# First norm rearranged, and the last down pair by seven block products: a hybrid encoder layer on one core

## The chip, the core and the metric

The kernel runs on one core of one Trainium2 chip. The metric is the device time of one execution in microseconds (us). TensorE (PE) does the matrix products into PSUM banks, VectorE (DVE) and ScalarE (ACT) do elementwise work and read the banks, GpSimd (POOL) does some elementwise work and issues some transfers, SyncE (SP) issues most transfers.

## What is computed

One step of an encoder layer for 512 prompt tokens and 64 sample tokens of running streams, 576 in all, with 1024 features. In short:

```
h = LN1(alpha*x + 0.5*FFN1(x))                    # FFN(x) = (silu(x@Wg) * (x@Wu)) @ Wdown, inner width 2816
z = h @ w_in                                       # mLSTM q,k,v,o,i,f | attention q,k,v | two branch gates
h = LN2(alpha*h + w_out(sig(g_m)*P_m(mLSTM(h)) + sig(g_a)*P_a(BandAttn(h))))
y = LN3(alpha*h + 0.5*FFN2(h))
LN(x) = (x - mean) * rsqrt(var + 1e-5) * g + b
```

i and f are the mLSTM's two gates, four heads each: eight columns of `w_in` in all. Attention goes over a band of earlier positions with a learned position bias. The new states of the streams are returned as well.

## The kernel before, in words

**Layout and precision.** Features lie on the 128 partitions, tokens along the free dimension, so the 576 tokens of one block of 128 features are a row of a tile (`T` = 576, `KT` = 8 blocks). Every operand of a matmul is split into a high part in the reduced format fp32r and a low part, the remainder; a product is three matmuls, wh·xh, wh·xl and wl·xh. The high part is a copy by ACT, the low part a subtraction by DVE. For the weights named in `ADDED`, and in some other places, `add_lo` makes the low part without DVE: ACT writes the negated high part, and a transfer issued by POOL adds the source to it. Tokens go in two halves, `HALVES`: 256 + 320 or 320 + 256 columns, or 288 + 288 where block products are used.

**Block products.** Gate/up products, pairs of column tiles (`Units` and its subclasses) and pairs of down tiles (`seven`) use a Strassen–Winograd scheme: a 2×2 block product by seven block products in place of eight. The sums of input blocks that it needs are made by DVE (`Combos`, `Inner`), the sums of weight blocks too (`split_ds`, `prep`). In `seven`, the 22 inner tiles of a down product are 8 (tiles 8 to 15) by block products and 14 by plain products (`plain`); `plan_ffn` lists the weights in the order in which they are loaded.

**Order.** PE's order is written out by hand: `od` counts model time with every group of matmuls (`tick`), and `later(dt, fn)` runs `fn` when that time has come. `od.bg` holds generators that are stepped every so many ns of model time. The other engines' instructions are placed by the scheduler with the priorities that the code gives (`hot`, `high_priority`, `issue_after`). The weights come through two raw buffers (`wr`) and four pairs of split ones (`NWB`).

**A norm.** `Norm.take` adds a product's bank to a tile of the residual `d[j]`, `last` adds tile and square to the running sums, `stats` sums these over partitions by matmuls, `rsqrt` takes the power on POOL, `centre` subtracts the mean from all eight tiles (those in `CP` on POOL), `spread` broadcasts the reciprocal deviation by a matmul and schedules `apply` for each tile: a scaling on DVE, the bias and the high part on ACT, the low part on DVE. The third norm's second half goes another way, transposed (`turned`).

**First norm and the columns after it.** FFN1's last pair of down tiles, 6 and 7, goes by `seven` with a function `first` in the middle, which closes the first half. Of the seven products three go one after the other into bank X, and DVE reads X between them. Then the first column tiles of `w_in` are multiplied in four passes (`WAVE_M`): tiles 0 to 2 of the list for the first half, tile 3, tiles 0 to 2 for the second half, tile 3. The list is 48, 40, 32 (first tiles of attention's v, k and q) and `if`, the gates' columns. They leave their banks as `vf`, `kf`, `qf` and, for the gates, by four ACT operations on 4 partitions (`gate_cb`). The gates' rows are then computed by `gate_rows`, a generator in `od.bg`, while the column pairs (`un.run`) are under way.

**Attention output.** `os_split` splits the attention output and makes the block sums for its projection; for the last three indices POOL begins them (`Combos.begin`), with the two subtractions.

**FFN2's last pair.** Tiles 6 and 7 go by four `gemm`s over all 22 inner tiles, one for each tile and half, and the weights are loaded and split once for each half; the third norm's `spread_at` is 4920.

## Time and profile before

| | us |
|---|---|
| median of 3 runs (lowest to highest) | 1553.24 (1552.8 to 1553.64) |
| the profiled execution | 1553.24 |
| its span in the profile | 1551.5 |
| PE busy | 1530.7 (99%) |
| DVE busy | 1140.2 (73%) |
| ACT busy | 891.7 (57%) |
| POOL busy | 234.7 (15%) |

The span runs from the first to the last recorded instruction. An engine is busy while it executes; waiting is not counted. In the timeline, a row gives the start in us, the busy time, the engine, the code line, the operation, out<-in with the names of tiles, partitions x elements, and how many instructions are joined; in brackets stands how long the engine was idle before it, and what ended that. Matmuls overlap, so a group's busy time is longer than its step, the distance from one start to the next. Line 152 is the helper for elementwise operations of two tiles, 155 the one with a scalar, 149 that for ACT, 135 that for matmuls. A row that begins with two times joined by a colon gives a stretch, its length, busy time and count of PE, PE's weight loads, DVE, ACT and POOL, the granted PE clock, the share of time in which the DMA engines are busy and GB/s.

### The profile page before, as it was taken

The numbers are of one execution on the slowest core, as the hardware profiler recorded it, in microseconds if no ns is written. First come the engines' busy times: TensorE is split into PE (matmuls) and PEld (weight loads), VectorE is DVE, ScalarE is ACT, GpSimd is POOL, SyncE is SP. The second block draws the span as 40 slices with busy tenths as digits, with TensorE's granted clock in tenths as the row PEclk, the third lists the DMA queues.
The fourth block names the chain that finished last, engine by engine and source line by source line (L and its number), as shares of the span: only waits on it lengthen the run. The fifth ranks groups of instructions, "written<-read, shape, count | busy, mean of one in ns | idle before, by whom it ended". The sixth has DMA issues, their size and how long they took to land.

```text
span 1551.5 us, 29498 instructions
## 1 busy us (share of the span) xinstructions
PE 1530.7 (99%) x11579; PEld 1516.1 (98%) x11579; DVE 1140.2 (73%) x2103; ACT 891.7 (57%) x1700; POOL 234.7 (15%) x437
## 2 busy tenths in 40 slices
PE   9999999999999999999999999999999999999998
PEld 9999999999899999999999999999999999999997
DVE  7877778675988766777586766755776877788756
ACT  7544457442866557777754877753456454457333
POOL 1000000000310015555311222202121000001000
PEclk9999999999999999999999999999999999999999
DMA  9232323533754438687534765642755323226334
GB/s 262 108 109 83 105 86 93 142 108 89 204 150 155 137 130 223 153 204 188 120 137 137 189 145 138 163 144 82 210 141 128 109 82 109 82 72 145 119 113 150
DMA packets 80260, 211.15 MB, mean 136 GB/s; under 512 B 9081, under 2 KB 20985, under 8 KB 80121
## 3 DMA queue, kind: packets, MB, share of 16 engines
q1 hardware_dynamic: 65144, 169.15, 33.3%
q0 software_dynamic: 11808, 34.28, 12.7%
q10 hardware_dynamic: 3168, 5.83, 1.1%
q8 instruction: 91, 1.49, 0.4%
q14 instruction: 49, 0.39, 0.1%
HBM read 172.27 MB, written 21.63 MB: 125 GB/s over the span
## 4 chain that ended last, share of the span: by engine, by line
PE 87%; DVE 4%; ACT 4%; DMA 2%; POOL 1%; issue 1%; SPq 0%; ACTq 0%; DVEq 0%; POOLq 0%
PE mm L135 70%; PE aux L135 15%; PE aux L145 2%; DVE s L152 1%; ACT sc L149 1%; DVE wl L152 1%; DVE sc L1585 1%; DMA s<-in_xT 1%; ACT s L149 1%; DMA G<-in_rbias 1%; ACT wh L149 0%; POOL kh L159 0%; DMA wr<-in_w_gu 0%; ACT wh L872 0%; DVE s L155 0%
## 5 line engine op out<-in xcount | busy, mean ns | idle before, releaser
L135 PE MATMUL mm<-s,wh 128*128 128x288 f32 (+2 forms) x3667 | 752.2, 298 | 6.9 <-DVE s L152 3.1
L135 PEld LDWEIGHTS mm<-s,wh 128*128 128x128 f32 x3667 | 588.0, 189 | 11.4 <-DVE s L152 2.3
L135 PE MATMUL mm<-s,wl 128*128 128x288 f32 (+2 forms) x1806 | 533.1, 295 | 0.0
L135 PEld LDWEIGHTS mm<-s,wl 128*128 128x128 f32 x1806 | 340.0, 188 | 0.0
L149 ACT ACTIVATE wh<-wr 128x1024 fp32r<-128x1024 f32 (+2 forms) x143 | 134.0, 948 | 156.7 <-PE mm L135 91.3
L152 DVE TENSOR_TENSOR wl<-wr,wh 128x1024 fp32r<-128x1024 f32 (+2 forms) x93 | 107.5, 1164 | 49.0 <-ACT wh L149 48.6
L135 PE MATMUL mm<-tx,wh 128*128 128x288 f32 x677 | 140.3, 296 | 0.8 <-DVE tx L152 0.8
L135 PEld LDWEIGHTS mm<-tx,wh 128*128 128x128 f32 x677 | 109.2, 188 | 1.2 <-DVE tx L152 1.0
L152 DVE TENSOR_TENSOR wl<-wt,wh 128x1024 fp32r<-128x1024 f32 x51 | 62.5, 1225 | 55.8 <-ACT wh L872 55.8
L135 PE MATMUL mm<-tx,wl 128*128 128x288 f32 x350 | 103.2, 295 | 0.0
L872 ACT ACTIVATE wh<-wt 128x1024 fp32r<-128x1024 f32 x51 | 54.1, 1060 | 83.1 <-DVE wt L152 83.1
L152 DVE TENSOR_TENSOR wl<-wu,wh 128x1024 fp32r<-128x1024 f32 x63 | 77.1, 1223 | 31.3 <-ACT wh L872 31.3
L872 ACT ACTIVATE wh<-wu 128x1024 fp32r<-128x1024 f32 x63 | 66.7, 1058 | 41.2 <-PE mm L135 34.3
L135 PE MATMUL mm<-tx,ah 128*128 128x288 f32 x416 | 85.4, 297 | 0.4 <-ACT st L149 0.4
L198 POOL DMA_DIRECT2D s<-s x16 | 13.7, 854 | 469.4 <-DVE hb L152 426.7
L149 ACT ACTIVATE h<-h 128x288 f32<-128x288 f32 x78 | 34.0, 436 | 60.9 <-DVE h L152 60.9
L135 PEld LDWEIGHTS mm<-tx,ah 128*128 128x128 f32 x416 | 66.2, 188 | 1.2 <-ACT st L149 0.6
L135 PEld LDWEIGHTS mm<-tx,wl 128*128 128x128 f32 x350 | 65.7, 188 | 0.0
L152 DVE TENSOR_TENSOR ws<-wu 128x1024 f32<-128x1024 f32 (+1 forms) x55 | 64.7, 1176 | 0.0
L152 DVE TENSOR_TENSOR wl<-ws,wh 128x1024 fp32r<-128x1024 f32 x51 | 62.2, 1219 | 3.0 <-ACT wh L872 3.0
L135 PE MATMUL mm<-h,wh 128*128 128x288 f32 (+2 forms) x304 | 62.7, 296 | 0.1
L135 PE MATMUL mm<-tx,al 128*128 128x288 f32 x208 | 61.1, 294 | 0.0
(398 smaller groups left out, 3481.8 us busy)
## 6 DMA issues: line engine op xcount, KB each, us to landing
wu<-in_w_gu SPq DMA_DIRECT2D x78, 512.0 KB, 4.4
wr<-in_w_in SPq DMA_DIRECT2D x48, 512.0 KB, 4.2
wr<-in_w_dn SPq DMA_DIRECT2D x37, 512.0 KB, 3.8
wl<-in_w_in POOLq DMA_DIRECT2D x36, 512.0 KB, 6.3
wu<-in_w_in SPq DMA_DIRECT2D x24, 512.0 KB, 4.5
wr<-in_w_dn SPq DMA_DIRECT2D x19, 384.0 KB, 3.2
s<-s POOLq DMA_DIRECT2D x16, 288.0 KB, 4.4
wu<-in_w_ap SPq DMA_DIRECT2D x8, 512.0 KB, 4.7
```

Source lines behind the costliest of these rows:

```text
L135: PE.matmul(out, lhsT, rhs, start=start, stop=stop, **kw)
L145: PE.transpose(out, in_, idn)
L149: return ACT.activation(out, in_, func, **kw)
L152: return (eng or DVE).tensor_tensor(out, a, b, op=op)
L198: return POOL.dma_start(lo, src, accum_op=ALU.add)
L872: self.last = ACT.activation(hi, src, AF.Copy)
L1585: DVE.tensor_tensor_reduce(out=out, in0=ps, in1=g, op0=ALU.add, op1=ALU.min, scale=1.0, scalar=3e38, accum_out=acc)
```

## The change

1. `seven` for FFN1's last pair takes the same order as the others up to q0·t3; a22·t4 goes into a bank R of its own, with one more `take`. The plan of its weights changes to fit.
2. `CP` is empty: all of `centre` on DVE, in all norms.
3. `spread` sets 650 in place of 860 between the tiles of the third norm, the final one; the other norms keep 860.
4. Column tile 32 is last in plan and list; `if` takes its place among the first three; its low part is made by `add_lo`.
5. The first two loads of the column pairs go through `later`.
6. `gate_rows` starts at 30000 in place of 50000, with its first operation behind `un.lo`, a low half of the pairs' weights.
7. `os_split`: all block sums on DVE; three of the eight low halves by `add_lo`.
8. FFN2's last pair goes by `seven` over eight inner tiles, and one `gemm` over the other 14 for both tiles and halves, with the weights held; `spread_at` is 3000.

```diff
-    PIECES = {("in", 48), ("in", 40), ("in", 32)}
+    PIECES = {("in", 48), ("in", 40)}
-    ADDED = {("in", c + j) for c in (32, 40, 48) for j in range(2, KT)} | {("in", c) for c in (*range(2, 8), *range(10, 32), *range(56, 72))} \
+    ADDED = {("in", 32)} | {("in", c + j) for c in (32, 40, 48) for j in range(2, KT)} | {("in", c) for c in (*range(2, 8), *range(10, 32), *range(56, 72))} \
-    CP = (6, 7)
+    CP = ()
...
-            seven(6, "vu")
+            seven(6)
             chunk(6, 0)
             chunk(6, 2)
             return
-        for r in range(2):
-            for j in (6, 7):
-                for c in range(3):
-                    chunk(j, c)
+        seven(6)
+        for j in (6, 7):
+            chunk(j, 0)
+            chunk(j, 2)
...
-    plan_in((48, 40, 32))
+    plan_in((48, 40))
     plan.append(("if", ins["w_if"]))
+    plan_in((32,))
...
-                later(860 * j, lambda j=j: self.apply(j, hf, rb))
+                later((860 if self.final is None else 650) * j, lambda j=j: self.apply(j, hf, rb))
...
-        def begin(self, i):
...
@@ seven
-        if first is None:
-            product(Z, "q1", "t1", True)
-            ln.take(j + 1, B, Z, ALU.subtract)
+        product(Z, "q1", "t1", True)
+        ln.take(j + 1, B, Z, ALU.subtract)
         product(X, "q0", "t3", False, "v")
         ln.take(j + 1, B, X, ALU.subtract)
         if first is None:
             product(Z, "t1", "b22", False, "t")
-        product(X, "a22", "t4", False, "u" if first is None else None)
-        ln.take(j + 1, A, X, ALU.subtract)
-        if first is not None:
+            product(X, "a22", "t4", False, "u")
+            ln.take(j + 1, A, X, ALU.subtract)
+        else:
+            R = bank()[:, :HT_]
+            ln.take(j + 1, A, X, ALU.subtract)
+            product(R, "a22", "t4", True, "u")
+            ln.take(j + 1, A, R, ALU.subtract)
             first()
-            product(Z, "q1", "t1", True, "u")
-            ln.take(j + 1, B, Z, ALU.subtract)
             product(Z, "t1", "b22", False, "t")
...
@@ ffn, the last pair for n == 2
-                    for hf in range(2):
-                        ln.residual(6, hf)
-                    for j, hl in [(j, (hf,)) for hf in (0, 1) for j in (6, 7)]:
-                        gemm([[((f"dn{n}", j, c), nk) for c, (_, nk) in enumerate(DC)]], hp_, [ln.cb(j)], (((0,), hl),))
+                    ln.spread_at = 3000
+                    Y, Z = seven(n, 6, inner, ln)
+                    for ps, cc in ((Y, A), (Z, B)):
+                        ln.take(6, cc, ps, ALU.add)
+                    for j in (7, 6):
+                        ln.whole(j)
...
+                    gemm([[((f"dn{n}", j, c), DC[c][1]) for c in (0, 2)] for j in (6, 7)], Outer(), [ln.cb(j) for j in (6, 7)],
+                         (((0,), (0,)), ((1,), (0,)), ((0,), (1,)), ((1,), (1,))))
...
     def gate_rows():
-        yield stt(t1, fx, -1.0, fx, ALU.mult, ALU.max)
+        with tc.issue_after(un.lo.ins):
+            first = stt(t1, fx, -1.0, fx, ALU.mult, ALU.max)
+        yield first
...
-    un.load(0)
-    un.load(1)
+    for i in range(2):
+        later(8000 + 2500 * i, lambda i=i: un.load(i))
...
-    gemm([[(("in", 48), KT)], [(("in", 40), KT)], [(("in", 32), KT)], [("if", KT)]], H,
-         [out_cb(vf0, "v", 0), out_cb(kf0, "k", 0), q0_cb, gate_cb], WAVE_M)
+    gemm([[(("in", 48), KT)], [(("in", 40), KT)], [("if", KT)], [(("in", 32), KT)]], H,
+         [out_cb(vf0, "v", 0), out_cb(kf0, "k", 0), gate_cb, q0_cb], WAVE_M)
...
-        later(50000, lambda: od.bg.append((GR, gate_rows())))
+        later(30000, lambda: od.bg.append((GR, gate_rows())))
...
@@ os_split
                     act(hi, t)
-                    tt(lo, t, f(hi), ALU.subtract)
+                    if n or i == 3:
+                        tt(lo, t, f(hi), ALU.subtract)
+                    else:
+                        add_lo(lo, hi, t)
...
                 for i in range(4):
-                    if i == 0:
-                        combos.sums[0] = slot(F32)
-                    if i < 3:
-                        combos.sums[2 * i + 2] = slot(F32)
-                        combos.begin(i + 1)
-                    combos.add(i, i > 0)
+                    combos.sums[2 * i] = slot(F32)
+                    combos.add(i)
```

Three places show how the order moves. PE, in `seven` for FFN1's last pair, where t0·t2 has just gone into X (`mm_607`). Before, the next products are q0·t3 and a22·t4, here their border:

```order
L135 MATMUL mm_607_4342<-s_488_3291,wh_604_4304 128x288
L135 MATMUL mm_607_4342<-s_489_3292,wh_604_4304 128x288
L135 MATMUL mm_607_4342<-s_488_3291,wl_605_4305 128x288
L135 MATMUL mm_607_4342<-s_454_3156,wh_609_4347 128x288
L135 MATMUL mm_607_4342<-s_455_3157,wh_609_4347 128x288
L135 MATMUL mm_607_4342<-s_454_3156,wl_610_4348 128x288
```

After the change, the same place and the twelve rows behind it (Z is `mm_608`, the new bank `aux_615`):

```order
L135 MATMUL mm_608_4343<-s_488_3291,wh_604_4304 128x288
L135 MATMUL mm_608_4343<-s_489_3292,wh_604_4304 128x288
L135 MATMUL mm_608_4343<-s_488_3291,wl_605_4305 128x288
L135 MATMUL mm_607_4342<-s_456_3161,wh_609_4347 128x288
L135 MATMUL mm_607_4342<-s_457_3162,wh_609_4347 128x288
```

```order
L135 MATMUL mm_607_4342<-s_488_3291,wl_610_4348 128x288
L135 MATMUL aux_615_4420<-s_454_3156,wh_604_4304 128x288
L135 MATMUL aux_615_4420<-s_455_3157,wh_604_4304 128x288
L135 MATMUL aux_615_4420<-s_454_3156,wl_605_4305 128x288
```

Z's product now stands between two that go into X, and a22·t4 starts a bank that nobody reads.

ACT, where the column tiles' first half leaves its banks, between the norm's second half (`s` rows: bias, high part). Before:

```order
L149 ACTIVATE s_3587<-s_3587,cols 128x288
L149 ACTIVATE vf_647_4623<-mm_4675 128x256
L149 ACTIVATE s_4583<-s_3587 128x288
L149 ACTIVATE kf_648_4624<-mm_4682 128x256
L1677 ACTIVATE qf_649_4625<-mm_4692 128x256
L149 ACTIVATE s_3040<-s_3040,cols 128x288
```

After:

```order
L149 ACTIVATE s_4670<-s_3038 128x288
L149 ACTIVATE vf_643_4610<-mm_4656 128x256
L149 ACTIVATE kf_644_4611<-mm_4665 128x256
L149 ACTIVATE li<-mm_4675 4x256
L149 ACTIVATE rows<-mm_4675 4x256
L149 ACTIVATE fx<-mm_4675 4x256
L149 ACTIVATE t_4598<-mm_4675 4x256
L149 ACTIVATE s_3587<-s_3587,cols 128x288
```

In place of `qf` the third bank is emptied by the gates' four operations, and two normalisations have moved behind them.

DVE, in the third norm, around the take of the last product (`mm_19019`) of the kernel; the rows with `cols` are the scalings of the first half. Before:

```order
L155 SCALAR_TENSOR_TENSOR s_17568<-s_17568,cols,aux_19005 128x320
L155 SCALAR_TENSOR_TENSOR s_18117<-s_18117,cols,aux_19005 128x320
L155 SCALAR_TENSOR_TENSOR s_18119<-s_18119,cols,aux_19005 128x320
L152 TENSOR_TENSOR s_18119<-mm_19019,s_18119 128x256
L155 SCALAR_TENSOR_TENSOR var_19145<-aux_19114,m_2884_19146 128x2
```

After:

```order
L155 SCALAR_TENSOR_TENSOR s_17572<-s_17572,cols,aux_19023 128x320
L155 SCALAR_TENSOR_TENSOR s_18121<-s_18121,cols,aux_19023 128x320
L152 TENSOR_TENSOR s_18123<-mm_19019,s_18123 128x256
L155 SCALAR_TENSOR_TENSOR s_18123<-s_18123,cols,aux_19023 128x320
L155 SCALAR_TENSOR_TENSOR s_19125<-aux_19089,m_19117,s_18930 128x512
```

The last scaling of the first half has moved behind the take.

18 lines of the change are left out of this document (7 added, 11 removed).

## The prediction

> **What bounds the kernel now.** I read the page's busy times first, then TensorE's waits by releaser, then single stretches of the timeline. PE is busy in all but 20.8 of 1551.5 us, so only two things can shorten the kernel: fewer or shorter matmuls, and less waiting on PE.
>
> ```profile
> span 1551.5 us, 29498 instructions
> PE 1530.7 (99%) x11579; PEld 1516.1 (98%) x11579; DVE 1140.2 (73%) x2103; ACT 891.7 (57%) x1700; POOL 234.7 (15%) x437
> ```
>
> The profiled execution took 1553.24 us, which is also the median of the three runs; 1.7 us lie around its span. The sum is made against it. TensorE's waits (what it waited for, us in total, times, longest) name the places that the change touches:
>
> ```profile
> PE mm L135 <- DVE s L152: 3.3, 5, 1.2
> PE mm L135 <- ACT vf L149: 1.5, 1, 1.5
> PE mm L135 <- DVE st L155: 1.4, 1, 1.4
> ...
> PE mm L135 <- ACT st L149: 0.4, 1, 0.4
> PE aux L135 <- DVE s L152: 0.4, 1, 0.4
> ```
>
> The first two lines are the first norm, `st` the gates' rows beside the column pairs, the last the statistics of the last norm; 0.8 more stand at the split of the attention output, below. Together 7.8 us: no rearranging at these places can bring more.
>
> **First norm: own bank.** The rows are in order of time: PE's two waits, and what DVE did before them.
>
> ```profile
> 377.32 1.23 DVE L152 TENSOR_TENSOR wl<-wr,wh 128x1024 fp32r<-128x1024 f32 x1
> 378.46 0.45 DVE L152 TENSOR_TENSOR s<-s,mm 128x288 f32<-128x288 f32 x1
> ...
> 379.06 0.50 PE L135 MATMUL mm<-s,wh 128*128 128x288 f32 x2 [1.21 <-DVE s L152]
> ...
> 380.93 0.45 DVE L152 TENSOR_TENSOR s<-s,mm 128x288 f32<-128x288 f32 x1 [1.65 <-PE mm L135]
> ...
> 381.53 0.50 PE L135 MATMUL mm<-s,wh 128*128 128x288 f32 x2 [0.64 <-DVE s L152]
> ```
>
> Twice PE adds the next product into bank X only after DVE has read X; the first read stands behind a weight split of 1.23. The new order puts q1·t1 into Z between them and a22·t4 into a bank of its own, so 1.21 + 0.64 = 1.85 go. One more `take` (0.45) lies beside matmuls. What is late next is the norm itself: the products end earlier, but the column matmuls need the normalised tiles.
>
> **First norm: subtractions, fourth tile.** Around the first column matmul:
>
> ```profile
> 387.55 1.43 DVE L152 TENSOR_TENSOR s<-s,c 128x288 f32<-128x288 f32 x2
> ...
> 387.68 1.98 POOL L152 TENSOR_TENSOR s<-s,c 128x288 f32<-128x288 f32 x2
> ...
> 389.00 0.97 DVE L152 TENSOR_TENSOR s<-s,sq 128x288 f32<-128x288 f32 x1
> ...
> 391.09 1.55 DVE L152 TENSOR_TENSOR s<-s,c 128x288 f32<-128x288 f32 x4
> 392.57 0.93 DVE L155 SCALAR_TENSOR_TENSOR s<-s,cols,aux 128x288 f32<-128x288 f32 x2
> ...
> 395.91 0.39 PE L135 MATMUL mm<-s,wh 128*128 128x256 f32 x1 [1.07 <-DVE s L152]
> ```
>
> Four undisturbed subtractions take 1.55, so one costs about 0.37 where they follow each other. Beside POOL's pair two DVE instructions take 1.0 each where 0.45 is usual. Moving the pair to DVE costs 2 × 0.37 = 0.74 and frees about 1.1: +0.3 at most. But all eight subtractions, and the split of the gates' 64 columns (512 elements, by an estimate 0.37 × 512/288 = 0.66; it comes earlier now), stand ahead of the first scaling. Laying the changed order out at these durations I get that scaling again at 392.6 and the first low half at 395.5 instead of 395.9: of 1.85 + 1.07 only 0.4 survives, the rest becomes waiting for DVE.
>
> The second half of the pass is where I expect a loss:
>
> ```profile
> 408.27 1.72 PE L135 MATMUL mm<-s,wh 128*128 128x256 f32 x13
> ...
> 411.11 0.36 ACT L149 ACTIVATE vf<-mm 128x256 f32<-128x256 f32 x1
> ...
> 411.52 0.56 PE L135 MATMUL mm<-s,wh 128*128 128x320 f32 x2 [1.53 <-ACT vf L149]
> ...
> 411.96 0.37 ACT L1677 ACTIVATE qf<-mm 128x256 f32<-128x256 f32 x1
> ```
>
> PE is through at 409.99 and waits until ACT, behind its normalisations, has evacuated `vf`. In the new order one more 128x1024 operation on ACT (el, by an estimate from the 256-column rows about 1.1) lies ahead of `vf`, which I find evacuated just before 411.3; that covers the late last low half (seven subtractions ahead of it on DVE, near 406.8, a wait of 1.3 inside the pass before). Only where this pass starts counts: 411.3 for 411.5 is all that is left of the stalls, +0.2. Then the third bank is the gates', with four ACT evacuations behind `kf` instead of one. From 411.11 to 411.96 lie three operations, 0.28 each; five more end at about 412.8. The third tile's matmuls are wanted six of 0.146 after the start, at 412.2, and wait 0.6. Sum: 0.2 − 0.6 = **−0.4 us**. Its ends: all four stalls go (1.85 + 1.07 + 1.53 = +4.4), or the 1.3 is not covered (−0.4 − 1.3 = −1.7). I stay near the lower end because DVE is what ended last at three of the four places, and it gets more work. The raw load of the fourth tile's weights waits for its buffer until about 391; its cover is the columns before it, whose last pass ends at 410. Loads of the first units, issued later on SP now, are wanted after all of these columns: nothing.
>
> **Gates' rows.**
>
> ```profile
> 447.19 3.09 DVE L155 SCALAR_TENSOR_TENSOR t<-t,t 4x576 f32<-4x576 f32 x4
> 450.21 1.21 DVE L152 TENSOR_TENSOR wl<-ws,wh 128x1024 fp32r<-128x1024 f32 x1
> 451.34 0.43 DVE L155 SCALAR_TENSOR_TENSOR st<-st,mm 128x288 f32<-128x288 f32 x1
> ```
>
> Four of the gates' operations on 4 partitions take 3.09 us, then a weight split 1.21, and only then comes the subtraction that frees a bank: PE waits 1.4. The other wait, 0.4 for ACT's `st`, has the gates' last rows ahead of it on ACT. The change starts the generator at 30000 instead of 50000, but its first operation now waits for a weight split of the units (`un.lo`), and the order shows its rows further back, between the units, one to three at a time. 1.4 + 0.4 = 1.8 go; what the same 0.75 us operations cost elsewhere I bound by nothing and by once more the 1.4. DVE is idle for a quarter of the span, so I take 0.3: **+1.5 us** (0.4 to 1.8). One more activation table load on ACT (24 for 23 in the order) lies beside this.
>
> **Split of the attention output.** POOL's six subtractions go to DVE, and three of eight low halves go from DVE to an ACT negation and an accumulating transfer issued by POOL.
>
> ```profile
> 784.00:803.00 19.00, 18.21 (x134) 17.76 (x133) 17.91 (x28) 10.30 (x18) 4.20 (x4) 1.00 0.18 59
> ...
> 792.31 1.06 DVE L155 SCALAR_TENSOR_TENSOR o<-s,o 128x288 f32<-128x288 f32 x1
> ...
> 795.12 1.04 DVE L155 SCALAR_TENSOR_TENSOR o<-s,o 128x288 f32<-128x288 f32 x1 [0.70 <-POOL s L152]
> ...
> 800.08 0.75 DVE L152 TENSOR_TENSOR tx<-o,tx 128x576 fp32r<-128x576 f32 x1
> ...
> 800.89 0.40 PE L135 MATMUL mm<-tx,wh 128*128 128x288 f32 x1 [0.79 <-DVE tx L152]
> ...
> DMA to landing us min/median/max: 3.5/5.8/7.7
> ```
>
> PE waits for the low half that ends at 800.83. DVE loses three low halves (3 × 0.67) and about 1.2 + 0.7 of waiting for POOL, and gets 6 × 0.37 = 2.2; but the last index's four additions now stand behind the read of the second product's bank, which depends on ACT's queue, with three weight additions of about 0.6 (512 elements) between them. From that read, which I put at 797.3 by ACT's new order: 0.36 + 4 × 0.37 + 3 × 0.6 + 0.75 = 4.4, so 801.7, 0.9 later. Then the transfers: the last is issued near 798, and its tile is wanted near 803. The row gives the landing of all transfers into `tx` tiles; near its lower end the data are there at 802, at the median 0.7 late, at the longest 2.6 late. The DMA engines are quiet here, 0.18 of their time in the first row, the last but one of its numbers, so 0.1: **−1.0 us** (−3.5 to +0.8, the wait as a whole). [...]
>
> **Last down pair.**
>
> ```profile
> 356.48 5.92 PE aux L135 x45
> ...
> 1504.91 17.32 PE mm L135 x118
> ...
> 1523.39 1.23 DVE wl L152
> ...
> 1525.08 1.48 PE aux L135 x8
> ...
> 1532.75 8.13 PE mm L135 x69
> ...
> 1528.59 3.87 DVE L152 TENSOR_TENSOR s<-s,c 128x320 f32<-128x320 f32 x6 [2.28 <-ACT c L149]
> ...
> 1536.31 2.83 DVE L155 SCALAR_TENSOR_TENSOR s<-s,cols,aux 128x320 f32<-128x320 f32 x6
> ...
> 1540.91 0.42 DVE L152 TENSOR_TENSOR s<-mm,s 128x256 f32<-128x256 f32 x1 [1.78 <-PE mm L135]
> ```
>
> The chain's pieces give a matmul's step: 0.1316 at 288 columns, 0.1468 at 320, 0.1178 at 256. Before, both tiles take 22 inner tiles × 3 products in both halves: 132 × 0.1468 + 132 × 0.1178 = 34.9. After: 7 block products of 12, and 84 in each half over 14 inner tiles: 84 × 0.1316 + 84 × 0.1468 + 84 × 0.1178 = 33.3. That is +1.6. The weight split of 1.23, behind which the statistics start at 1525.08, is gone from there (both tiles' weights are held): +0.4, the last of PE's waits above. But the second half has 84 matmuls (9.9 us) to cover the first half's normalisation, where it had 132 (15.5). Counted from the statistics' start, with the same 15 or so done by then: 69 × 0.1178 + 1.48 for the statistics + about 0.5 for the broadcast puts PE's end at 10.1. DVE starts subtracting at 3.5 (1528.59 − 1525.08), then eight subtractions of 0.40 (0.37 × 320/288; before, POOL had two), 1.0 for the other tile's take and sums, seven scalings of 0.46 (their closer spacing, 650 for 860, puts them ahead of the last take in the order): 10.9 before that take. DVE waited 1.78 for PE there; now PE's result waits 0.8: −0.7 with rounding. **+1.4 us** (0.6 if the broadcast comes late as well, 2.1 if the take slips ahead). The additional `whole`, takes and four weight additions of the block products lie beside 11 us of matmuls, on a DVE that has eight weight splits there for twelve. Second norm (all subtractions on DVE): of PE's 3.3 us for `s` the three waits shown are 2.9, so no more than 0.4 can lie there; nothing, ±0.4.
>
> **Sum.** −0.4 + 1.5 − 1.0 + 1.4 = +1.5: 1553.24 − 1.5 = 1551.7 us, 0.1% faster, which a measurement of this kernel can't tell from no change; 0.2% (3.1 us) is the bound for that.
>
> **Rivals.** (1) The first norm's stalls do go: its products end 1.85 earlier, and DVE, free of POOL, keeps up, because the hand order errs by some tenths at each of a dozen hand-overs. For it speaks that 4.4 of PE's idle time lies there, against it that DVE has no idle time in any row from 387.55 to 392.57. With about half of the stalls (+2.4 for −0.4) it gives 1548.9, with all 1546.9. (2) The accumulating transfers land late. In the split that is 2.6 instead of 0.1; in the first norm the fourth tile's low half now comes by one too, issued near 398 and wanted near 407.3:
>
> ```profile
> DMA to landing us min/median/max: 5.3/6.4/10.1
> ```
>
> At its longest that is 408.1, 0.8 late. Together 3.3 more: 1555.0. It makes the kernel slower than before as soon as the two places lose 1.5 more, by the split alone at a landing of 6.7 us; for 0.2% it needs 4.6 more, some 9 us there, longer than any in its row. For it: nothing behind the last transfer hides it; against it: the 0.18. (3) The tail gives only 0.6 and the gates' rows stall elsewhere, 0.4: 1551.7 + 0.8 + 1.1 = 1553.6, no change.
>
> **Chances.** Forecast 0.52, (1) 0.30, (2) 0.10, (3) 0.08. Faster by over 0.2% is below 1550.1: nearly all of (1), 0.27, and 0.05 of the forecast's own spread, 0.32. Slower is above 1556.4: 0.03 of (2), where the first norm is at its lower end too, and 0.05 of the forecast's, where several terms are at theirs: 0.08. The rest, 0.60, is no change. The range reaches from 1547.8 (three quarters of the first norm's stalls) to 1555.0 (the transfers' longest landing).
>
> **What would show it.** Right: PE's waits before the 288-column products at 379 and 381 gone; a wait of some 0.6 at the third tile of the 320-column pass; none of 1.4 for `st`; PE's wait for `tx` about 1.7, twice what it was before; 12 matmuls fewer, and the last take waiting for DVE, not PE. Wrong: first low half of the columns ready before 394.5 (rival 1), PE waiting on a DMA near 803 (rival 2), or `st` among PE's releasers again (rival 3).

## Result, and the profile after

The changed kernel takes 1559.33 us (median of 5 runs, 1557.57 to 1560.77), the kernel before 1553.64 beside it (5 runs, 1552.80 to 1554.07): a ratio of 1.0036, 95% interval 1.0025 to 1.0047. It is slower, outside the range, where 1551.7 was forecast. One run of e4_hi_first (1850.41) and one of the kernel before (1846.79), both at a granted clock of 0.75, are left out of all figures below. The profiled execution took 1560.17 us, 6.9 more than the one before. Its page:

```profile
span 1558.3 us, 29454 instructions
PE 1536.3 (99%) x11567; PEld 1521.9 (98%) x11567; DVE 1138.1 (73%) x2120; ACT 891.8 (57%) x1700; POOL 223.1 (14%) x425
```

PE has 12 matmuls fewer and is busy 5.6 us longer. That can't come from waits, which are not busy time. The view by stretches shows it in the granted clock, the third number from the end. The kernel before:

```profile
394.00:397.40 3.40, 2.32 (x17) 1.89 (x16) 3.40 (x10) 2.52 (x7) 3.27 (x4) 1.00 0.97 355
397.40:407.60 10.20, 9.92 (x76) 9.15 (x75) 8.30 (x21) 8.13 (x18) 4.30 (x7) 1.00 0.60 218
...
807.00:810.40 3.40, 3.40 (x28) 3.40 (x27) 2.71 (x4) 1.75 (x3) 0.00 (x0) 1.00 0.22 47
```

The changed one:

```profile
394.00:397.40 3.40, 1.48 (x8) 1.07 (x8) 2.55 (x8) 1.72 (x4) 1.74 (x3) 1.00 0.97 323
397.40:407.60 10.20, 9.56 (x41) 9.07 (x42) 4.68 (x12) 7.50 (x20) 1.81 (x2) 0.50 0.71 218
...
804.00:807.00 3.00, 0.41 (x2) 0.20 (x2) 2.96 (x6) 0.68 (x1) 0.00 (x0) 1.00 0.65 139
807.00:810.40 3.40, 3.40 (x14) 3.40 (x15) 1.79 (x3) 1.93 (x3) 0.00 (x0) 0.50 0.34 87
...
1547.70:1551.00 3.30, 3.30 (x18) 3.30 (x18) 1.77 (x4) 0.33 (x3) 0.70 (x1) 0.50 0.40 140
```

In three places PE, kept waiting, comes back at half its clock: 41 matmuls in 10.2 us where there were 76, 14 in 3.4 where there were 28. Before, the clock is 1.00 up to 1546.88, beyond the last product (done at 1544.4). TensorE's waits after the change:

```profile
PE mm L135 <- ACT s L149: 3.5, 2, 2.2
PE mm L135 <- ACT tx L149: 2.5, 1, 2.5
...
PE aux L135 <- DVE s L152: 0.9, 2, 0.5
PE mm L135 <- DVE tx L152: 0.9, 1, 0.9
...
PE mm L135 <- ACT st L149: 0.6, 2, 0.4
...
PE mm L135 <- ACT t L149: 0.6, 1, 0.6
```

Of the waits quoted before, DVE's 3.3 for `s` has shrunk to 0.3, ACT's 1.5 for `vf` and DVE's 1.4 for `st` are gone. Two long waits on ACT stand in their place. The timeline of the first norm:

```profile
394.49 0.43 ACT L149 ACTIVATE s<-s 128x288 fp32r<-128x288 f32 x1
...
394.97 0.38 PE L135 MATMUL mm<-s,wh 128*128 128x256 f32 x1 [2.19 <-ACT s L149]
...
396.59 1.06 ACT L149 ACTIVATE wh<-wr 128x1024 fp32r<-128x1024 f32 x1 [1.68 <-DMA wr<-in_w_in]
397.56 0.43 ACT L149 ACTIVATE s<-s 128x288 fp32r<-128x288 f32 x1
...
398.04 1.07 PE L135 MATMUL mm<-s,wh 128*128 128x256 f32 x2 [1.31 <-ACT s L149]
...
399.76 2.55 PE L135 MATMUL aux<-onec,s 128*128 128x1 f32 x12
```

ACT's split of column tile 32 (396.59) waits for its load, with the norm's next high half (397.56) behind it; PE waits for that, at half clock by now. In the attention output the place is this:

```profile
797.53 0.84 POOL L198 DMA_DIRECT2D tx<-s  x1 [3.00 <-ACT tx L149]
...
802.77 0.46 DVE L152 TENSOR_TENSOR s<-o 128x288 f32<-128x288 f32 x1 [1.75 <-DMA tx<-s]
...
804.97 0.68 ACT L149 ACTIVATE tx<-o 128x576 fp32r<-128x576 f32 x1 [2.55 <-DVE o L155]
...
805.71 0.40 PE L135 MATMUL mm<-tx,wh 128*128 128x288 f32 x1 [2.55 <-ACT tx L149]
806.99 0.61 PE L135 MATMUL mm<-tx,wh 128*128 128x288 f32 x1 [0.88 <-DVE tx L152]
```

DVE may write its next block sum only when an accumulating transfer is done with the old one in that slot. The one issued at 797.53 landed at 802.74, 5.2 us later: 1.75 lost, then DVE, ACT and PE in turn. And at the end:

```profile
1546.32 0.42 DVE L152 TENSOR_TENSOR s<-mm,s 128x256 f32<-128x256 f32 x1
...
1546.79 0.61 PE L135 MATMUL aux<-onec,s 128*128 128x1 f32 x4 [0.51 <-DVE s L152]
...
1547.94 1.95 PE L145 MATMUL aux<-ident,s 128*128 128x128 f32 x8
1549.68 1.74 PE L145 MATMUL mm<-ident,s 128*128 128x128 f32 x8
```

The same two groups of transposes took 1.07 and 1.04 before.

All experiments are read with one table, the distances in us between six marks of PE in each profile: a product inside FFN1's down pairs, the first 320-column product of the column tiles, a transpose of the attention near 760, its first `qk` product near 970, the first product of FFN2's last pair, its last 256-column product, and the end of the span.

| profile of | first norm | columns, gates | output split | to last pair | last pair | tail |
|---|---|---|---|---|---|---|
| before | 74.53 | 347.76 | 211.03 | 495.89 | 74.39 | 10.94 |
| after | 77.83 | 347.57 | 215.31 | 495.23 | 72.26 | 13.07 |
| e1_list_back | 77.27 | 349.49 | 215.68 | 495.41 | 72.27 | 12.21 |
| e4_hi_first | 76.19 | 347.27 | 215.19 | 495.40 | 72.27 | 12.22 |
| e2_split_back | 77.03 | 347.84 | 211.59 | 495.43 | 72.26 | 12.22 |
| e5_bank_back | 77.41 | 347.64 | 214.62 | 496.40 | 72.26 | 13.23 |
| e6_fill | 74.87 | 347.61 | 215.99 | 495.40 | 72.26 | 12.20 |
| e7_lo_dve | 75.75 | 348.12 | 214.82 | 495.44 | 72.26 | 13.14 |
| e8_three_back | 73.11 | 348.16 | 211.69 | 495.40 | 72.27 | 11.31 |
| e9_norm_back | 74.51 | 346.86 | 216.91 | 495.83 | 72.26 | 13.65 |
| e10_two_kept | 74.54 | 347.75 | 211.09 | 495.93 | 72.26 | 13.22 |
| e11_cp_back | 75.96 | 347.14 | 217.18 | 495.91 | 72.26 | 13.70 |
| e3_spread_late | 77.69 | 347.69 | 215.49 | 495.25 | 72.26 | 11.30 |
| e12_eight_fill | 72.77 | 350.13 | 211.31 | 495.42 | 72.26 | 11.31 |
| e13_sums_back | 75.45 | 349.05 | 215.88 | 495.29 | 72.26 | 12.21 |
| e14_eight_list | 75.55 | 347.13 | 211.12 | 495.41 | 72.26 | 11.30 |
| e15_pool_first | 74.53 | 346.76 | 211.07 | 495.26 | 72.25 | 11.30 |

Profiles whose instructions in a stage are the same show how far a single one can be trusted. The changed kernel's first norm stands in five (after, e2, e3, e7, e13): 75.45 to 77.83, with half clock for one period of 3.4 us or for three. Its output split stands in eight (after, e1, e3, e4, e5, e6, e9, e11): 214.62 to 217.18, with one or two. Its tail stands in eight (after, e1, e2, e4, e5, e6, e7, e13): 13.07 to 13.23 where the clock fell ahead of the transposes, 12.20 to 12.22 elsewhere. A difference between two profiles that lies inside such a range shows no effect of an edit.

### The profile page after: what moved, and what is told of

The parts are those of the page before. It is cut to its first block, busy times and chain, and to the rows that moved or that the text cites. A ratio compares the mean times of both kernels' runs of the same rounds, so it can differ in the third digit from the quotient of the medians.

```text
span 1558.3 us, 29454 instructions
## 1 busy us (share of the span) xinstructions
PE 1536.3 (99%) x11567; PEld 1521.9 (98%) x11567; DVE 1138.1 (73%) x2120; ACT 891.8 (57%) x1700; POOL 223.1 (14%) x425
## 3 DMA queue, kind: packets, MB, share of 16 engines
q0 software_dynamic: 12384, 35.69, 13.1%
## 5 line engine op out<-in xcount | busy, mean ns | idle before, releaser
L135 PEld LDWEIGHTS mm<-s,wh 128*128 128x128 f32 x3691 | 594.2, 189 | 9.1 <-ACT s L149 3.9
L149 ACT ACTIVATE wh<-wr 128x1024 fp32r<-128x1024 f32 (+2 forms) x137 | 129.0, 952 | 147.1 <-PE mm L135 73.0
L152 DVE TENSOR_TENSOR wl<-wr,wh 128x1024 fp32r<-128x1024 f32 (+2 forms) x86 | 100.8, 1181 | 42.8 <-ACT wh L149 42.6
L864 ACT ACTIVATE wh<-ws 128x1024 fp32r<-128x1024 f32 x51 | 53.7, 1054 | 9.5 <-PE mm L135 8.3
```

The costliest lines, as they stand in the source:

```text
L135: PE.matmul(out, lhsT, rhs, start=start, stop=stop, **kw)
L149: return ACT.activation(out, in_, func, **kw)
L152: return (eng or DVE).tensor_tensor(out, a, b, op=op)
L864: self.last = ACT.activation(hi, src, AF.Copy)
```

## Experiments

The theory: PE's waits did not grow much, they gathered in fewer places; a place empty enough is followed by a stretch at half clock, and those stretches are the loss. The rivals: one part of the change is simply late (the order of the list, the bank, the transfers), and taking it out brings the time back. Ratios are to the kernel before, run in turn on the same chip (its medians: 1553.7 to 1554.2).

**When the clock falls** (p_probe: the kernel before, with stalls put into FFN2's gate/up products; it computes the same).

```diff
+    def stall(k):
+        mm(ps, one_, one_, True, True)
+        for _ in range(k):
+            DVE.tensor_copy(ps, ps)
+        mm(ps, one_, one_, True, True)
```

> The kernel before, with TensorE made to wait at eight points of FFN2's gate/up units, where it otherwise never waits: a small product into a spare bank, a chain of 3 to 18 copies of that bank on DVE, and a product that needs the last copy. Clock theory: the granted TensorE clock falls to half a few us after a wait of about 2 us or more (the changed kernel's two drops came after waits of 2.2 + 0.3 + 1.3 and of 2.5 + 0.9 us within 5 us) and stays there for some 3.4 us or a multiple; waits of up to 1.5 us leave it at 1.00, as all of the kernel before do. Each wait beyond the threshold then costs 1.7 us or more on top of its own length. Rival (waits alone): the clock stays at 1.00 at all eight points, and the span grows by the waits' lengths only.

One run, 1621.04 us. The stalls came out longer than planned, 2.2 to 7.3 us (the author's guess is that DVE had other work ahead of the copies). All but the shortest were followed by half clock, those of 2.35 and 2.88 among them. The shortest was not (the timeline of PE):

```profile
1236.52 0.49 PE L135 MATMUL aux<-one 128*128 128x128 f32 x2 [2.21 <-DVE aux L776]
```

It is as long as the 2.19 in the changed kernel that was. So length alone doesn't decide. In the traces the clock changes on a grid of 3.413 us (in the changed kernel at 397.41, 407.65, 807.01, 810.43, 1547.71 and 1551.12, the last five 3, 120, 121, 337 and 338 periods behind the first); laid over this wait, the grid cuts it (busy shares 0.47 and above 0.8 on the two sides), where the end of the 2.19, the 0.28 behind it and the start of the 1.31 leave 0.43 of one period. Over the 18 profiles of this study, of the periods at full clock that begin between 20 and 1548 us, with the next one still inside the span: of 29 that were busy for 0.44 or less, all 29 were followed by half clock; of 16 between 0.44 and 0.60, six; of those above, only six, busy for 0.85 to 0.92 with twelve to fifteen of the statistics' one-column products in them; without these, five of the six hold 0.33 to 0.44.

**Is it the place of column tile 32?** e1_list_back takes the old list and its old low half by DVE; e4_hi_first keeps the new list and puts ACT's split of tile 32 behind the third normalised tile.

```diff
-    PIECES = {("in", 48), ("in", 40)}
+    PIECES = {("in", 48), ("in", 40), ("in", 32)}
-    gemm([[(("in", 48), KT)], [(("in", 40), KT)], [("if", KT)], [(("in", 32), KT)]], H,
+    gemm([[(("in", 48), KT)], [(("in", 40), KT)], [(("in", 32), KT)], [("if", KT)]], H,
```

> The changed kernel with the list of the first column tiles as before: 48, 40, 32, gates, and tile 32's low part by DVE. Clock theory: its split, which waits on ACT for a raw load ahead of the second tile's high part, no longer holds TensorE; the two waits of 2.2 and 1.3 us shrink below 1.5, the clock stays up, and about 4.5 us come back: 1554.5 to 1555.5. Rival (waits alone): only 1 to 1.5 us come back, since the first norm's waits before the change add up to as much: about 1558.

1560.29, ratio 1.0041 [1.0026, 1.0056]: nothing came back. The waits have run together into one, behind ACT's split of the gates' weights, which waits 3.56 for its load, and three periods of half clock follow:

```profile
397.09 1.11 PE L135 MATMUL mm<-s,wh 128*128 128x256 f32 x2 [3.51 <-ACT s L149]
```

```diff
+                                tc.issue_after(HI[-1].ins) if plan[c][0] == ("in", 32) else nullcontext():
```

> The changed kernel with the list as changed, but tile 32's split placed on ACT behind the third normalised tile's high part. If the split's place on ACT is the cause, the 1.3 us wait at the second tile goes; the 2.2 us at the first, which waits for DVE, stays. Clock theory: with one wait left in the stretch the clock stays up or falls for one 3.4 us period only: 1554.5 to 1557. Rival (waits alone): 1558.

1558.58, ratio 1.0031 [1.0020, 1.0043]. The wait of 1.31 is gone and the clock is low for one period instead of three, but PE waits 0.90 at 403.17 and 0.85 at 409.30 instead: first norm 76.19. That isn't shown to be the edit's doing. 76.19 lies inside the 75.45 to 77.83 of the unedited order, and in e2, e7 and e13 the wait of 1.31 is missing too, since ACT waits there only 0.58 to 0.90 for that load.

**The split of the attention output.** e2_split_back undoes it; e7_lo_dve gives the low halves back to DVE and keeps all sums there; e13_sums_back gives POOL its sums back and keeps the transfers.

```diff
-                    combos.add(i)
+                    if i < 3:
+                        combos.sums[2 * i + 2] = slot(F32)
+                        combos.begin(i + 1)
+                    combos.add(i, i > 0)
-                        add_lo(lo, hi, t)
+                    tt(lo, t, f(hi), ALU.subtract)
```

> The changed kernel with the split of the attention output as before (POOL begins the block sums, all low halves on DVE). Clock theory: the waits of 2.5 and 0.9 us go back to 0.8 to 1, and 3.4 us at half clock go with them: 4.3 us less, 1555.0. Rival (waits alone): 2.6 us less, 1556.7.

1554.59, ratio 1.0001 [0.9992, 1.0011]: 4.7 us back, and the clock stays at 1.00 there. The stretch is 211.59 again.

```diff
-                    if n or i == 3:
-                        tt(lo, t, f(hi), ALU.subtract)
-                    else:
-                        add_lo(lo, hi, t)
+                    tt(lo, t, f(hi), ALU.subtract)
```

> The changed kernel with all low halves of the attention output's block sums on DVE; the sums stay on DVE, without POOL. If the accumulating transfers are the cause (each holds its source tile until it lands, and the next sum on DVE waits for that tile), the waits of 2.5 and 0.9 us shrink to 1 to 1.8 together, the clock stays up there, and 3 to 4 us come back: 1555.5 to 1556.5. Rival (DVE lacks POOL's help): three more low halves on DVE, the wait grows: 1559 to 1560.

1559.50, ratio 1.0038 [1.0025, 1.0051]. Without any transfer DVE is nearly as late by itself: PE waits 2.09 and 0.88, where 1 to 1.8 together was to show the transfers as the cause, 3.4 with them. The last sum and the high half behind it:

```profile
803.28 0.45 DVE L155 SCALAR_TENSOR_TENSOR o<-o,o 128x288 f32<-128x288 f32 x1
...
803.76 0.68 ACT L149 ACTIVATE tx<-o 128x576 fp32r<-128x576 f32 x1 [2.03 <-DVE o L155]
```

> The changed kernel with POOL beginning three of the block sums of the attention output again; three of its eight low halves still come by accumulating transfers. Theory A (DVE has too much to do in this place once all sums are its own): the waits of 2.6 and 0.9 at 805 us within 1.2 in sum, clock 1.00 there, the stretch from 762 to 977 us 211.0 to 212.0 as before, 1555. Theory B (the transfers land 3.4 to 6.1 us after their issue and hold the tile that the next sum is to be written into; who makes the sums is second): waits as in the changed kernel or longer, stretch 214 to 216, 1559.

1559.07, ratio 1.0034 [1.0021, 1.0046]; PE waits 1.89 and 0.80. Now POOL's sums stand in its queue behind the issue of a transfer:

```profile
795.60 0.84 POOL L198 DMA_DIRECT2D tx<-s  x1 [1.52 <-ACT tx L149]
796.80 0.82 POOL L152 TENSOR_TENSOR s<-o 128x288 f32<-128x288 f32 x1 [0.36 <-issue]
...
797.65 1.05 DVE L155 SCALAR_TENSOR_TENSOR o<-s,o 128x288 f32<-128x288 f32 x1 [3.39 <-POOL s L152]
```

Each half of this part alone is enough for the loss; only without both is the stretch 211 to 212.

**The first norm: bank, subtractions, all of it.** e5_bank_back takes the old order of FFN1's last pair:

```diff
-            R = bank()[:, :HT_]
...
-            product(R, "a22", "t4", True, "u")
-            ln.take(j + 1, A, R, ALU.subtract)
+        product(X, "a22", "t4", False, "u" if first is None else None)
+        ln.take(j + 1, A, X, ALU.subtract)
```

> The changed kernel with FFN1's last pair in its old order, three products in bank X. Clock theory: the change's own bank gathers three waits of 1.2, 0.6 and 1.1 us into one of 2.2 us within one 3.4 us period of the clock's grid; undone, no period in the first norm falls below a busy share of 0.45, the clock stays at 1.00 there, and 3.5 to 4 us come back: 1555.5. Rival (the norm's length decides): the products end 1.9 us later again, so the time gets worse by up to 1.9 or stays: 1559 to 1561.

1559.26, ratio 1.0035 [1.0022, 1.0048]: the expectation failed. e8_three_back is the same program up to the attention output, with that as before and `spread_at` 4920:

```diff
-                    ln.spread_at = 3000
+                    ln.spread_at = 4920
```

> The changed kernel with the old order of FFN1's last pair, the old split of the attention output, and the last norm's scalings later (4920), so that the last take doesn't stand behind seven of them. Left of the change: subtractions on DVE, the fourth tile, the gates' rows, the last pair by block products. Clock theory: no drop before the last us; 3.7 + 4.3 + 2 us come back: 1549 to 1550.5, faster than before by 3 to 4.5 (gates' rows 1.3, last pair 2.1). Rival (waits alone): 1553 to 1555.

1553.93 over ten runs, ratio 0.9999 [0.9989, 1.0008]; they fall into two groups, 1550.9 to 1551.9 (four) and 1553.7 to 1555.8 (six). The profiles of these two kernels are the cleanest pair of the study, since both have the same instructions here. e5_bank_back:

```profile
396.19 0.38 PE L135 MATMUL mm<-s,wh 128*128 128x256 f32 x1 [1.50 <-ACT s L149]
397.16 0.38 PE L135 MATMUL mm<-s,wh 128*128 128x256 f32 x1 [0.58 <-DVE s L152]
...
399.79 2.55 PE L135 MATMUL aux<-onec,s 128*128 128x1 f32 x12
```

e8_three_back:

```profile
396.65 0.38 PE L135 MATMUL mm<-s,wh 128*128 128x256 f32 x1 [1.50 <-ACT s L149]
397.62 0.38 PE L135 MATMUL mm<-s,wh 128*128 128x256 f32 x1 [0.58 <-DVE s L152]
...
399.48 1.39 PE L135 MATMUL aux<-onec,s 128*128 128x1 f32 x12
```

The waits agree to 0.01 us; the grid lies differently (a period from 394.13, busy for 0.39, in the one; one from 395.91, busy for 0.61, in the other), and the first norm takes 77.41 or 73.11. That is 4.3 us for the phase of the clock's grid alone. The mean clock of the runs goes with the groups (0.998 and 0.999 in the lower, 0.995 to 0.998 in the upper), though one run of 1555.3 shows 0.998, which this doesn't explain.

> The changed kernel with CP (6, 7) again: two of the eight subtractions of each half of a norm on POOL. Theory A (in the first norm ACT ends last: DVE waits 1.47 and 2.81 us for ACT there, so what DVE has to do less is not felt): wait of 2.2 at 395 us within 0.5, clock again at one half after it, 1558.8 to 1559.8. Theory B (the eight subtractions on DVE make the first scalings late, and all behind them): wait under 1.2, clock 1.00 there, 1555.5 to 1556.5.

```diff
-    CP = ()
+    CP = (6, 7)
```

1561.45, ratio 1.0049 [1.0036, 1.0062]: no gain; that it is worse than the changed kernel the intervals don't show. The wait is 1.93 and the clock still falls, as theory A says. In this profile two subtractions on POOL cost 0.7 on the way to the last pair (495.91 for 495.23) and 0.6 in the tail (13.70 for 13.07).

> The changed kernel with the whole first-norm group undone (FFN1's last pair in its old order, CP (6, 7), column tile 32 third with its low half by DVE, the units' loads where they were); split of the attention output, gates' rows and last down pair stay changed. Theory A (the group's parts together starve PE around 395 us, so that only undoing all of them brings back a first norm whose single waits are under 2 us and whose clock stays at 1.00): the 4.1 us of the changed kernel up to the gates' columns (3.3 to the 320-column pass, 0.74 at its third tile) come back, 1559.3 - 4.1 = 1555.2, granted clock 1.00 up to 800 us; the drop at 804 us stays. Theory B (the time lost there is not made by this group but comes from elsewhere, the later loads or the other norms' subtractions): 1558.5 or more, as with each part undone alone.

The edits are those of e1_list_back, e5_bank_back and e11_cp_back together, and the units' loads where they were. The first norm is back at 74.51 and the columns at 346.86, as expected (3.3 + 0.7 us), but the time is 1559.11, ratio 1.0025 [1.0009, 1.0041], not 1555.2: in the output split the clock was low for two periods instead of one (216.91 for 215.31), and the tail with `CP` (6, 7) and spread 3000 takes 13.65. The parts don't add up: the same split takes 214.62 to 217.18 in the eight profiles named above, with one period at half clock or two.

**Filling the wait.** e6_fill is the changed kernel with 22 products that nobody reads in the gap of 2.2 us; e12_eight_fill is e8_three_back with 14.

```diff
+    warm = bank()[:, :P]
+    for _ in range(22):
+        mm(warm, ones_r, ones_r, True, True)
```

> The changed kernel with 22 products of a constant 128x128 tile into a spare bank ahead of the first column tile, where TensorE waits 2.2 us anyway; their result isn't used. Clock theory: the wait is filled, the period is busy, the clock stays at 1.00 through the first norm, and 3 to 4 us come back though work is added: 1555.5 to 1556.5. Rival (waits alone): no gain, 1559 to 1560, or worse where the filling runs past the wait.

1558.12, ratio 1.0027 [1.0018, 1.0036]. More work for PE, and yet the first norm is shorter (74.87) than in any of the five profiles without the filling, by 0.6 to 3.0; half clock for one period, whose predecessor holds twelve one-column products. The intervals don't separate the whole time from the changed kernel's, so the 3 to 4 us expected are not shown.

> The version with three parts back (old order of FFN1's last pair, old split of the attention output, spread_at 4920) and 14 products of the ones tile with itself, read by nobody, ahead of the first column tile: they fill the wait of 1.5 us there. Theory A (the two groups of that version, 1550.9 to 1551.9 and 1553.7 to 1555.8, have the same instructions and waits and differ by the clock alone, which falls when a period of 3.4 us holds too little work): one group, granted clock 1.00 up to 1546 us, 1551.2, although nothing is taken from the wait. Theory B (the second group is made by something else, late transfers for instance, or the remaining wait of 0.58 with one-column products in the same period is enough for a drop): two groups as before, median near 1554.

1552.85 (1551.68 to 1553.84, 11 runs), ratio 0.9993 [0.9984, 1.0002]: the two groups of e8_three_back are gone, the runs lie in one spread between them, with the clock at 1.00 around 395 us and the shortest first norm, 72.77. The intervals of the two versions overlap. The median stayed above 1551.2, for PE now comes to the gates' tile earlier than ACT, and that wait makes a half-empty period (0.44) of its own:

```profile
413.71 0.85 PE L135 MATMUL mm<-s,wh 128*128 128x320 f32 x4 [1.92 <-ACT t L149]
```

**The tail.** e3_spread_late is the changed kernel with `spread_at` 4920 alone.

> The changed kernel with spread_at 4920 in place of 3000 in the third norm: the last take ahead of the first half's scalings again. Theory A (the wait of 0.51 us for the last take's sum, and the clock at one half in the 3.4 us behind it, cost 2.2 at the end): 1557.2 and granted clock 1.00 behind 1545 us. Theory B (the scalings put off end the kernel later instead): 1559.0 to 1561.

1558.31, ratio 1.0027 [1.0016, 1.0039]: tail 11.30 for 13.07, 1.8 of the 2.2, and no wait at the statistics. Half of it, 0.9, is the clock, since the same tail takes 12.2 where the clock stays up.

e10_two_kept is the kernel before with the gates' rows and the last down pair of the change, and 4920:

```diff
+        with tc.issue_after(un.lo.ins):
-        later(50000, lambda: od.bg.append((GR, gate_rows())))
+        later(30000, lambda: od.bg.append((GR, gate_rows())))
+                    ln.spread_at = 4920
+                    Y, Z = seven(n, 6, inner, ln)
```

> The kernel before with two parts of the change alone: the gates' rows earlier, and the last down pair by seven block products with spread_at 4920 in place of 3000. Theory A (parts that take PE's waits away keep their gain, since no single wait gets long enough for a lower clock): gates' rows 1.24, last pair 2.1 from the profile of the changed kernel up to its last full matmul: 1553.7 - 3.3 = 1550.4, all runs in one group, granted clock 1.00 to 1540 us. Theory B (the tail gives back what the last pair gains, 0.8 to 2.1, since the last scalings come later): 1551.5 to 1552.5. Theory C (the phase of the clock's periods splits the runs also here): two groups some 3 us apart.

1552.19 (1551.35 to 1553.79, 11 runs), ratio 0.9993 [0.9984, 1.0001]: theory B. The last pair's 2.1 are given back by the tail, for with two subtractions on POOL it takes 13.22 even at 4920, where it takes 11.31 with all of them on DVE (e8_three_back):

```profile
1540.20 0.60 PE L135 MATMUL aux<-onec,s 128*128 128x1 f32 x4 [0.45 <-DVE s L152]
```

So `CP` has to be empty in the tail and in the second norm (0.5), but what does it do in the first? e14_eight_list is e8_three_back with the list of e1_list_back.

> The version with three parts back, and the list 48, 40, 32, if as well, with tile 32's low half by DVE: of the first norm's changes only the empty CP and the later loads stay. Theory A (the waits of the first norm are then spread as before, none of its periods is half empty): first norm's stretch to the 320-column pass 74.5 or a little less, gates' rows 0.9, second norm 0.5, last pair 2.1, tail back by 0.4: 1553.7 - 3.1 = 1550.6, one group. Theory B (all eight subtractions on DVE gather the waits in one place, whatever the list is): a wait of 1.5 or more ahead of the first column tile, a lower clock in part of the runs, two groups, median 1552 to 1554.

1552.12 (11 runs), ratio 0.9989 [0.9980, 0.9998]. Theory B, though the runs don't fall into two groups: the list is the old one, yet the waits gather ahead of the first column tile,

```profile
397.03 0.38 PE L135 MATMUL mm<-s,wh 128*128 128x256 f32 x1 [1.68 <-ACT s L149]
398.03 0.52 PE L135 MATMUL mm<-s,wh 128*128 128x256 f32 x1 [0.62 <-DVE s L152]
```

a period busy for 0.33, and half clock behind it. Its two shortest runs, 1550.61 and 1551.07, are those with a mean clock of 0.999. The later loads, which it also keeps, are not told apart from the subtractions.

**The version that follows.** All the stages' gains, and the first norm as it was, with its waits apart:

```diff
-                    tt(dh, dh, mb, ALU.subtract, POOL if j in CP else DVE)
+                    tt(dh, dh, mb, ALU.subtract, POOL if j in CP and self.gi == 0 else DVE)
```

> The kernel before with four parts: gates' rows earlier, last down pair by seven block products, spread_at 4920, and the subtractions of the second and third norm all on DVE, those of the first norm shared with POOL as before. Theory A (each part keeps what its stage showed, since no stage has a wait of more than 1.6 us any more: gates' rows 0 to 0.9, second norm 0.5, last pair 2.1, tail back by 0.4): 1553.9 less 2.2 to 3.1, 1550.8 to 1551.7, granted clock 1.00 up to 1546 us, all runs within 1.5 us. Theory B (the waits of 1.1 and 1.5 us in the first norm, which stay, fall badly in the clock's periods in part of the runs, though those of the kernel before don't show it): two groups, median above 1552.

1551.05 (1550.07 to 1552.08, 11 runs) against 1554.09, ratio 0.9981, interval 0.9972 to 0.9990: faster than both kernels, at theory A's time, with the clock at 1.00 up to 1546.5 us; the runs spread over 2.0 us, not 1.5. Its page, and the stretches of the first norm:

```profile
span 1549.1 us, 29447 instructions
...
PE 1529.8 (99%) x11567; PEld 1516.4 (98%) x11567; DVE 1138.8 (74%) x2114; ACT 889.2 (57%) x1697; POOL 230.0 (15%) x431
```

```profile
395.00:398.40 3.40, 2.32 (x17) 1.88 (x16) 3.40 (x10) 2.50 (x8) 3.27 (x4) 1.00 0.98 337
398.40:408.60 10.20, 9.94 (x75) 9.16 (x75) 8.31 (x21) 8.13 (x19) 4.30 (x7) 1.00 0.62 224
```

PE waits more in the first norm here than in the changed kernel (74.53 holds four waits of 0.6 to 1.5), but in no period for long.

## Why the prediction was wrong

**The step that failed**, behind all three terms that lost, is that a wait was priced at its own length, and a matmul at one duration for its width. The forecast looked at PE's waits and never asked what the clock does behind them, although the profile's page has a row for it. The half-clock stretches cost about 3.7 in the first norm (3.3 measured, where the waits alone would have given 0.4 less than before: 4.3 us of them for 4.7), 1.6 in the output split (4.28 less the 2.6 by which the waits grew) and 0.9 in the tail (13.1 to 13.2 with the drop, 12.2 without, same instructions). That is 6.2 of the 6.8 by which the span grew, in this profile; others of the same instructions lost less or more. e8_three_back against e5_bank_back shows such a cost with nothing else changed. Of the six signs that were to show the forecast right five came, all but the wait for `tx`, and none of the six looked at the clock.

**First norm, −0.4 forecast, −4.0 measured** (3.3 to the 320-column pass and 0.7 at its third tile, 0.6 forecast there). Without the half clock it is about −0.3, and the working held: the waits at the 288-column products near 379 and 381 went, the first scaling came at 392.74 (worked out: 392.6), and the first low half was done at 395.58 (395.5). PE's long wait of 2.19 names ACT, but ACT's high half hangs on that scaling, for which ACT itself had waited 2.85:

```profile
392.74 0.93 DVE L155 SCALAR_TENSOR_TENSOR s<-s,cols,aux 128x288 f32<-128x288 f32 x2
...
393.29 0.96 ACT L149 ACTIVATE s<-s,cols 128x288 f32<-128x288 f32 x2 [2.85 <-DVE s L155]
```

So DVE ended last there, as forecast. The wait of 1.31 was ACT's own, with a weight split in its queue that waited 1.68 for a load. The sentence that costed tile 32's load at nothing, its cover the columns before it, looked at who needs the weights, and not at who stands behind the split on ACT.

**Gates' rows, +1.5 forecast, about +0.9 measured.** The 1.4 for `st` went; of ACT's `st` two waits of 0.2 to 0.4 came elsewhere. The columns' stretch less the 0.7 at the third tile gained 0.9 in the changed kernel; it gained 1.0 in e15_pool_first, 0.9 in e9_norm_back, nothing in e10_two_kept. Its end at a transpose is no sharp mark: 347.57 and 349.05 (e13) belong to the same instructions.

**Split of the attention output, −1.0 forecast, −4.3 measured.** Rival 2 had the right suspect and the wrong place. PE does not wait for a transfer's data; DVE waits 1.75 to overwrite what the transfer still reads, which the working, with a DVE that waited only for the second product's bank, had no line for. DVE with all the sums is too late also without transfers: 3.0 of waiting for PE in e7_lo_dve, 3.4 with them, twice the 1.7 that was to show the step right.

**Last pair, +1.4 forecast, 0.0 measured.** Matmuls and statistics gave 2.1 for 2.0. The last take behind the scalings, priced at 0.7, kept PE waiting 0.51 at the statistics. The tail lost 2.1 all the same: 0.4 also with `spread_at` 4920 (11.30), 0.9 more with 3000, and 0.9 by the clock.

**Second norm, 0 forecast, +0.5 to +0.7 measured**, which the empty `CP` made: the kernels with `CP` (6, 7) stand at 495.8 to 495.9, those without at 495.2 to 495.4, all but one (e5_bank_back, 496.4, for which no run here gives a reason).

But for the clock, the first norm and the last pair came within 0.6 of their terms, the gates' rows and the second norm within 0.7, and the split missed by 1.6; together that is some 0.6 us slower, no change. "Slower", at 0.08, came about by a mechanism that was not among the rivals. The lower end of the range, 1547.8, comes out at 1548.0 by its own terms; the result doesn't touch it.

In the changed kernel's trace the granted clock is 1.00 or 0.50, and its changes lie 3.413 us or a multiple apart. Its wait of 2.19 was followed by half clock, the 2.21 of p_probe was not; the emptier of the periods that they fell into were busy for 0.43 and 0.47. Here it was how full a period was, and not how long a gap was, that went with the clock.

## What to carry to other kernels

When PE's busy time grows while its work shrinks, read the granted clock by stretches before anything else. PE's waits in the first norm before, spread over four places (1.21, 0.64, 1.07 and 1.53), cost their length, with the clock at 1.00 behind them; those of 2.19, 0.28 and 1.31, gathered within 5.3 us, cost up to 3.7 us on top. So a reordering that removes some waits and gathers the rest can lose, and its price is not fixed: two profiles of the same instructions, with the grid lying differently, were 4.3 us apart in the first norm. The accumulating transfers held the buffer that they read until they landed, 3.4 and 5.2 us after their issue, and DVE, which was to write it next, waited 0.41 and 1.75 for them. What the issuing engine had queued behind the issue waited as well: in e13_sums_back the issue waited 1.52 for ACT, POOL's sum came behind it, and DVE waited 3.39 for that sum.

## What was not expected of the hardware

- The clock's grid is 3.413 us (the changed kernel's stretches at half clock ahead of its end take 10.24, 3.41 and 3.41); 29 of 29 periods busy for 0.44 or less were followed by half clock, and of those above 0.60 only six, which held a dozen or more one-column products.
- Twelve to fifteen one-column products fill a period to 0.85 and more by the profile's count, and the clock still fell behind six such periods (after 1544.29 in the changed kernel for one). Periods like them whose other products alone held 0.47 or more were not followed by half clock, but for one (e6_fill).
- Products that nobody reads, put into a wait, went with a shorter stage: 74.87 for the first norm in e6_fill, 75.45 to 77.83 without them.
- Three accumulating transfers, each adding a 128x576 tile (288 KB), issued by POOL at 793.68, 797.53 and 801.41, landed after 3.4, 5.2 and 6.1 us. DVE waited 0.41 and 1.75 for the first two to write their sources again.
